# All streamed products with stationary weights, column tiles in pairs over two banks, and a feature-major residual

## The chip, the cores and the metric

One core of a Trainium2 chip runs the kernel. The metric is the device time of one execution in microseconds (us), smaller is better; the time shown is the median of three runs.

## What is computed

The kernel runs two layers on 256 tokens with 2048 features. Each layer is FFN, mixer, FFN, each on an RMS-normed input and added to the residual. The mixer of layer 0 (GDN) is a gated delta rule with 8 heads beside a multi-window pool; that of layer 1 (MLA) is latent attention with 16 heads.

```python
def swiglu(h, w_gate, w_up, w_down):
    return (jax.nn.silu(h @ w_gate) * (h @ w_up)) @ w_down
...
    for layer in range(DEPTH):
        x = x + 0.5 * swiglu(rms_norm(x, ffn1_norm[layer]), ffn1_w_gate[layer], ffn1_w_up[layer], ffn1_w_down[layer])
        h = rms_norm(x, mix_norm[layer])
        i = layer // 2
        if layer % 2 == 0:
            x = x + delta_pool_mixer(h, hyb_w_in[i], gdn_conv[i], gdn_a_log[i], gdn_dt_bias[i],
                                     gdn_out_norm[i], pool_w[i], pool_scale[i], hyb_w_out[i])
        else:
            x = x + mla_mixer(h, positions, mla_w_in[i], mla_q_norm[i], mla_kv_norm[i], mla_w_q_up[i],
                              mla_w_kv_up[i], mla_q_head_norm[i], mla_k_head_norm[i], mla_w_out[i])
        x = x + 0.5 * swiglu(rms_norm(x, ffn2_norm[layer]), ffn2_w_gate[layer], ffn2_w_up[layer], ffn2_w_down[layer])
```

The FFN width is 4096. All data are float32.

## The kernel before

Every large product is made in fp32r with both operands split: a high part (rounded to fp32r) and a low part (the rest), and three of the four partial products are summed: high with high, weight high with activation low, weight low with activation high. The weights stream from HBM in 1 MB slabs, `raw` (SyncE's queue, three buffers). `piece` makes of 1024 columns a high part on ScalarE (`whi`, a cast, L174) and a low part on VectorE (`wlo`, a subtraction, L175), with four buffers each.

There are two kinds of product. In the FFN and in the mixers' output projections (`columns`, `rows`) the activations are stationary: for each of 16 or 32 input tiles k and each 512 output columns there are six matmuls 512 wide (three partial products, two blocks of 128 tokens, one PSUM bank for each block). The results are token-major, and so is the residual `x[j]`, four tiles of [128, 2, 512]. Since the next product wants features on the partitions, PE transposes the FFN's hidden values (L458, eight per 512 columns) and, for the next norm, the residual (L336). In the mixers' input projections (`gemm`, `mm3`) the weights are stationary: for each k and 128 output columns there are three matmuls 256 wide into one bank, and the results are feature-major. `SKEW` and `PAD` set the distance of these operands' addresses.

The norm's gain is applied as `xg` is written (L158 on ScalarE and L159 on VectorE, high and low part). The factor 1/rms is taken from sums of squares that ScalarE accumulates per token (L309), and is applied to the results: as a per-token scale `r2` in the FFN (L134, L451), as the tile `R` in the mixers, made by one small matmul (`end_norm`).

A scheduler orders the instructions of each engine by a model of when each is ready, so the order on an engine is not the order of the code. Chains of small steps (heads, transposes) are spread between the streamed matmuls by a clock that counts PE's work (`ch.poll`, `LAG`).

Of the kernel before, what the change touches and what calls it, by code (L numbers as in the profile page):

```python
# [18 lines left out]
P = 128  # L19
# [6 lines left out]
PAD = 288  # L26
SKEW = 16
# [72 lines left out]
class Builder:  # L100
    def __init__(self, ctx, tc, ins, out):
        self.ctx, self.tc, self.nc, self.i, self.out = ctx, tc, tc.nc, ins, out
        self.act_set = None
        self.last_table = None
        pool = lambda name, bufs, **kw: ctx.enter_context(tc.tile_pool(name=name, bufs=bufs, **kw))
        self.cst = pool("cst", 1)
        self.xp = pool("xp", 1)
        self.wp = pool("wp", 4)
        self.tp = pool("tp", 2)
        self.ps = pool("ps", 1, space=PSUM)  # L110
        self.n = 0
        self.skew = 0
        self.ch = Chains()
# [52 lines left out]
    def piece(self, raw, h, step=1024):  # L166

        hi, lo = (
            self.wp.tile([P, 1024 + 64], F32R, tag=tag, bufs=4, name=self.nm(tag))[:, self.skew : self.skew + 1024]
            for tag in ("whi", "wlo")  # L170
        )
        for c in range(0, 1024, step):
            src, d = raw[:, h + c : h + c + step], slice(c, c + step)
            self.last_cast = self.nc.scalar.copy(hi[:, d], src)  # L174
            self.nc.vector.tensor_tensor(lo[:, d], src, hi[:, d].bitcast(F32), op=ALU.subtract)  # L175
        return hi, lo

    def weights(self, *aps):

        for ap in aps:  # L180
            n = ap.shape[1]
            for s0 in range(0, n, 2048):
                sz = min(2048, n - s0)
                raw = self.raw_tile()
                self.nc.sync.dma_start(raw[:, :sz], ap[:, s0 : s0 + sz])
                for h in range(0, sz, 1024):
                    yield self.piece(raw, h)
# [7 lines left out]
    def gemm(self, ps, stream, acts, wide=True):  # L195

        K = len(acts)
        for k0 in range(0, K, 8):
            self.gemm_piece(ps, next(stream), acts, k0, wide)

    def gemm_piece(self, ps, piece, acts, k0, wide=True):
        hi, lo = piece
        for k in range(k0, k0 + 8):
            w = slice((k - k0) * P, (k - k0 + 1) * P)
            self.ch.wait(lambda: acts[k] is not None)
            self.last_mm = self.mm3(ps, hi[:, w], lo[:, w], acts[k], k == 0, k == len(acts) - 1, wide)
            self.ch.poll()

    def mm3(self, ps, wh, wl, act, first, last, wide):
        if wide:  # L210
            if last:
                self.mm(ps[:, 0:256], wl, act[:, 0, :], start=False, stop=False)
            m = self.mm(ps[:, 0:512], wh, act.rearrange("p a t -> p (a t)"), start=first, stop=last)
            if not last:
                self.mm(ps[:, 0:256], wl, act[:, 0, :], start=False, stop=False)
        else:
            self.mm(ps[:, 0:256], wh, act[:, 0, :], start=first, stop=False)
            self.mm(ps[:, 0:256], wh, act[:, 1, :], start=False, stop=False)
            m = self.mm(ps[:, 0:256], wl, act[:, 0, :], start=False, stop=last)
        return m  # L220
# [56 lines left out]
    def warm_up(self):  # L277

        z = self.tmp([P, 512], "sq", 1)[:, 0:S]
# [6 lines left out]
    def load_rest(self):  # L286
        nc = self.nc
        nc.sync.dma_start(self.ca, self.i["ca"])
        self.behind(nc.scalar.copy(self.ones_r, self.ones), self.last_cast)
        for j in range(4):  # L290
            self.feed_squares(j, self.last_cast)
        self.norm_factor()

    def begin_norm(self, gain):
        self.gain = gain
        self.xg = [None] * KT
        self.ss = self.tmp([P, 2, 4], "ss", 2)

    def feed_part(self, d, src):

        t = self.xp.tile([P, 2, S], F32R, tag=f"xg{d}", name=self.nm("xg"))
        self.split_hi_lo(t, src, self.gains[:, self.gain, d : d + 1])
        self.xg[d] = t

    def feed_squares(self, j, earlier=None):

        for t in range(2):
            sq = self.tmp([P, 512], "sq", 1)
            a = self.nc.scalar.activation(sq, self.x[j][:, t, :], AF.Square, accum_out=self.ss[:, t, j : j + 1])  # L309
            if earlier is not None:  # L310
                self.behind(a, earlier)

    def norm_factor(self):

        nc = self.nc
        tot = self.tmp([P, 2], "tot", 1)
        nc.vector.tensor_reduce(tot, self.ss, axis=AX.X, op=ALU.add)
        self.r2 = self.tmp([P, 2], "r2", 1)
        self.rsqrt(self.r2, tot, 1.0 / D, True, "rt")
        self.dg = self.tmp([P, 2, P], "dg", 1)  # L320
        for t in range(2):
            nc.vector.tensor_scalar(self.dg[:, t, :], self.ident, self.r2[:, t : t + 1], None, op0=ALU.mult)

    def feed_norm(self, j):

        yield 1.2 * LAG
        self.feed_squares(j)
        if j == 3:
            self.norm_factor()
        x = self.x[j]  # L330
        for h in range(2):
            ps = self.psum("aux")
            for n in range(2):
                for t in range(2):
                    c = (2 * h + n) * P
                    self.nc.tensor.transpose(ps[:, (2 * n + t) * P : (2 * n + t + 1) * P], x[:, t, c : c + P], self.ident)  # L336
                    self.ch.clock += P / 2.4
            for n in range(2):
                self.feed_part(4 * j + 2 * h + n, ps[:, n * S : n * S + S])
            if h == 0:  # L340
                yield 0.5 * LAG

    def end_norm(self, after):

        ps = self.psum("aux")
        m = self.nc.tensor.matmul(ps[:, :S], self.ones, self.dg.rearrange("p a t -> p (a t)"), start=True, stop=True)
        self.behind(m, after)
        R = self.tp.tile([P, S], F32, tag="R", bufs=1, name=self.nm("R"))
        self.nc.scalar.copy(R, ps[:, :S])
        return R  # L350

    def rows(self, ps, hi, lo, act, first, last):

        blk = [slice(0, P), slice(P, 2 * P)]
        for part, w in ((0, hi), (0, lo), (1, hi)):
            end = last and part == 1
            for t in range(2):
                self.last_mm = self.mm(ps[t], act[:, part, blk[t]], w, start=first and w is hi and part == 0, stop=end)

    def columns(self, stream, acts):  # L360

        K = len(acts)
        ps = [self.psum("mm") for _ in range(2)]
        for k in range(K):
            if k % 2 == 0:
                piece = next(stream)
            hi, lo = (w[:, 512 * (k % 2) : 512 * (k % 2) + 512] for w in piece)
            self.ch.wait(lambda: acts[k] is not None)
            self.rows(ps, hi, lo, acts[k], k == 0, k == K - 1)
            self.ch.poll()  # L370
        return ps

    def project(self, slabs, acts, half, after):

        st = self.weights(*[slabs[j] for j in range(4)])
        for j in range(4):
            ps = self.columns(st, acts)
# [820 lines left out]
```

## Time and profile before

| | |
|---|---|
| median of three runs | 2829.64 us (2829.23 to 2829.73) |
| profiled execution | 2829.35 us, span 2827.3 us |
| PE busy | 2819.3 us of the span |
| DVE, ACT, POOL busy | 1555.1, 1360.2 and 57.4 us |
| granted clock | full in all 40 slices |
| read from HBM | 509.84 MB, 181 GB/s over the span |

PE is TensorE, DVE VectorE, ACT ScalarE, POOL GpSimd. Matmuls overlap on PE: the recorded time of one contains the filling of the array, so what a matmul costs is the distance from one start to the next (the pitch), not its recorded duration.

### The profile page before, as it was taken

The numbers are of one execution on the slowest core, as the hardware profiler recorded it, in microseconds if no ns is written. First come the engines' busy times: TensorE is split into PE (matmuls) and PEld (weight loads), VectorE is DVE, ScalarE is ACT, GpSimd is POOL, SyncE is SP. The second block draws the span as 40 slices with busy tenths as digits, with TensorE's granted clock in tenths as the row PEclk, the third lists the DMA queues.
The fourth block names the chain that finished last, engine by engine and source line by source line (L and its number), as shares of the span: only waits on it lengthen the run. The fifth ranks groups of instructions, "written<-read, shape, count | busy, mean of one in ns | idle before, by whom it ended". The sixth has DMA issues, their size and how long they took to land.

```text
span 2827.3 us, 35453 instructions
## 1 busy us (share of the span) xinstructions
PE 2819.3 (100%) x14398; PEld 2392.2 (85%) x14398; DVE 1555.1 (55%) x1893; ACT 1360.2 (48%) x1836; POOL 57.4 (2%) x97
## 2 busy tenths in 40 slices
PE   9999999999999999999999999999999999999999
PEld 8888888899998888888888888888999788888887
DVE  5445454576785545455454544545677555445444
ACT  6444444475465444444444444444578554444433
POOL 0000000000000000000000000000122000000000
PEclk9999999999999999999999999999999999999999
DMA  7555555545245555555555555555533455555554
GB/s 285 194 181 191 193 190 188 185 151 173 97 165 183 190 191 183 191 193 190 184 192 193 182 191 191 188 189 191 184 127 113 149 193 183 191 191 187 189 208 146
DMA packets 76500, 514.35 MB, mean 182 GB/s; under 512 B 10801, under 2 KB 11569, under 8 KB 15537
## 3 DMA queue, kind: packets, MB, share of 16 engines
q1 hardware_dynamic: 74464, 508.85, 52.5%
q8 instruction: 112, 1.84, 0.3%
q0 software_dynamic: 576, 2.10, 0.2%
q10 hardware_dynamic: 1296, 1.15, 0.1%
q14 instruction: 52, 0.42, 0.0%
HBM read 509.84 MB, written 2.10 MB: 181 GB/s over the span
## 4 chain that ended last, share of the span: by engine, by line
PE 98%; issue 1%; ACT 0%; DVE 0%; POOL 0%; DMA 0%; ACTq 0%; DVEq 0%; POOLq 0%
PE mm L193 91%; PE aux L193 4%; PE aux L458 1%; PE aux L336 1%; PE aux L701 0%; PE aux L1022 0%; PE aux L284 0%; ACT whi L174 0%; DMA cg<-in_cg 0%; ACT sq L309 0%; POOL osq L228 0%; PE aux L741 0%; ACT L129 0%; ACT sg L134 0%; ACTq L509 0%
## 5 line engine op out<-in xcount | busy, mean ns | idle before, releaser
L175 DVE TENSOR_TENSOR wlo<-raw,whi 128x1024 fp32r<-128x1024 f32 (+1 forms) x962 | 1175.2, 1222 | 1154.9 <-ACT whi L174 1153.4
L174 ACT CAST whi<-raw 128x1024 fp32r<-128x1024 f32 (+1 forms) x962 | 1007.9, 1048 | 1255.4 <-PE mm L193 1225.4
L193 PE MATMUL mm<-whi,xg 128*128 128x512 f32 x4096 | 1111.9, 391 | 0.0
L193 PEld LDWEIGHTS mm<-whi,xg 128*128 128x128 f32 x4096 | 764.3, 188 | 156.6 <-ACT whi L174 0.4
L193 PE MATMUL mm<-wlo,xg 128*128 128x512 f32 x2048 | 631.6, 389 | 0.0
L193 PE MATMUL mm<-whi,g 128*128 128x512 f32 x2048 | 554.8, 390 | 0.0
L193 PEld LDWEIGHTS mm<-wlo,xg 128*128 128x128 f32 x2048 | 384.4, 188 | 80.4 <-DVE wlo L175 0.4
L193 PEld LDWEIGHTS mm<-whi,g 128*128 128x128 f32 x2048 | 382.6, 188 | 78.0
L193 PE MATMUL mm<-wlo,g 128*128 128x512 f32 x1024 | 315.7, 389 | 0.0
L193 PE MATMUL mm<-xg,whi 128*128 128x256 f32 x1568 | 283.0, 283 | 0.6 <-ACT xg L158 0.5
L193 PEld LDWEIGHTS mm<-xg,whi 128*128 128x128 f32 x1568 | 239.9, 188 | 2.1 <-ACT xg L158 0.9
L193 PEld LDWEIGHTS mm<-wlo,g 128*128 128x128 f32 x1024 | 192.2, 188 | 40.3
L193 PE MATMUL mm<-xg,wlo 128*128 128x256 f32 x784 | 218.7, 279 | 0.0
L193 PEld LDWEIGHTS mm<-xg,wlo 128*128 128x128 f32 x784 | 148.3, 189 | 0.0
L193 PE MATMUL mm<-whi,o 128*128 128x512 f32 x256 | 72.3, 395 | 0.0
L228 POOL TENSOR_TENSOR sq<-sqf,sq 128x256 fp32r<-128x256 f32 x49 | 45.2, 928 | 1309.3 <-ACT sq L227 1296.3
L134 ACT ACTIVATE sg<-mm,r 128x512 f32<-128x512 f32 x64 | 40.6, 684 | 44.9 <-PE mm L193 44.9
L158 ACT ACTIVATE xg<-aux,gains 128x256 fp32r<-128x256 f32 x80 | 37.1, 471 | 36.9 <-DVE xg L159 26.2
L193 PEld LDWEIGHTS mm<-whi,o 128*128 128x128 f32 x256 | 47.0, 188 | 9.0
L462 ACT CAST g<-aux 128x512 fp32r<-128x512 f32 x64 | 37.3, 585 | 23.9 <-PE aux L458 23.9
L451 DVE SCALAR_TENSOR_TENSOR sg<-mm,r,sg 128x512 f32<-128x512 f32 x64 | 45.1, 746 | 5.8 <-PE mm L193 5.8
L159 DVE SCALAR_TENSOR_TENSOR xg<-aux,gains,xg 128x256 fp32r<-128x256 f32 x80 | 38.0, 481 | 16.6 <-ACT xg L158 16.6
(264 smaller groups left out, 1609.4 us busy)
## 6 DMA issues: line engine op xcount, KB each, us to landing
raw<-in_w1d SPq DMA_DIRECT2D x64, 1024.0 KB, 4.7
raw<-in_w2g SPq DMA_DIRECT2D x64, 1024.0 KB, 4.8
raw<-in_w2u SPq DMA_DIRECT2D x64, 1024.0 KB, 4.8
raw<-in_w2d SPq DMA_DIRECT2D x64, 1024.0 KB, 4.7
raw<-in_w1g SPq DMA_DIRECT2D x62, 1024.0 KB, 4.9
raw<-in_w1u SPq DMA_DIRECT2D x62, 1024.0 KB, 4.8
raw<-in_wqk SPq DMA_DIRECT2D x16, 1024.0 KB, 4.8
raw<-in_wgo SPq DMA_DIRECT2D x16, 1024.0 KB, 4.8
```

The lines of the kernel that those rows point to most:

```text
L134: a = nc.scalar.activation(out, in_, func, **kw)
L158: nc.scalar.activation(dst[:, 0, :], src, AF.Copy, scale=scale)
L159: nc.vector.scalar_tensor_tensor(dst[:, 1, :], src, scale, dst[:, 0, :].bitcast(F32), op0=ALU.mult, op1=ALU.subtract)
L174: self.last_cast = self.nc.scalar.copy(hi[:, d], src)
L175: self.nc.vector.tensor_tensor(lo[:, d], src, hi[:, d].bitcast(F32), op=ALU.subtract)
L193: return self.nc.tensor.matmul(out, lhsT, rhs, start=start, stop=stop)
L228: nc.gpsimd.tensor_tensor(dst[:, 1, :], sq, dst[:, 0, :].bitcast(F32), op=ALU.subtract)
L336: self.nc.tensor.transpose(ps[:, (2 * n + t) * P : (2 * n + t + 1) * P], x[:, t, c : c + P], self.ident)
L451: nc.vector.scalar_tensor_tensor(sg[:, t, :], ps[t], self.r2[:, t : t + 1], sg[:, t, :], op0=ALU.mult, op1=ALU.mult)
L458: nc.tensor.transpose(pt[:, (2 * n + t) * P : (2 * n + t + 1) * P], sg[:, t, c : c + P], self.ident)
L462: nc.scalar.copy(flat(0), pt)
```

## The change

All streamed products now keep the weights stationary. Two tiles of 128 output columns go together, A and B, each with a bank of its own. For each input tile k, `step` issues four matmuls: the high weights of A and of B against both parts of the activation at once (512 columns, parts side by side), then the low weights of A and of B against the high part (256 columns, into the first half of the bank); for the last k the low ones come first. High and low part of a piece lie 64 bytes apart in their tiles (`SIDE_A`, `SIDE_B`).

The halves of a bank are put together afterwards: `joined` copies one half to SBUF on ACT, adds the other on DVE and multiplies by `R` there. Results are feature-major everywhere, and so is the residual: 16 tiles of [128, 256], each updated by two DVE operations (`add_residual`). The transposes of hidden values and of the residual are gone, and with them the per-token scales. The sum of squares runs into a tile `acc`: for 14 of the 16 tiles on POOL (a multiplication and an addition each), for the last two on ACT and DVE; `end_norm` sums it over partitions by a matmul and takes the root of 128x256 values. In the opening of the first FFN, 256 gate and 256 up columns are made while the inputs arrive, where before it was 512 and 512; there the squares of six tiles run on POOL and of ten on ACT and DVE. The up-projections of the MLA heads (`wup`) go in pairs too, with two 512-wide casts per piece (`both_sides`), and the rotary parts of two pairs of heads are projected at once. The output is stored by ACT's DMA queue.

```diff
-PAD = 288
-SKEW = 16
+EXTRA = 64
+SIDE_A = (16, 0)
+SIDE_B = (0, 16)
+SIDE_V = (48, 48)
...
+    def split(self, hi, lo, src):
+        self.last_cast = self.nc.scalar.copy(hi, src)
+        self.nc.vector.tensor_tensor(lo, src, hi.bitcast(F32), op=ALU.subtract)
+    def piece(self, raw, h, side=SIDE_A):
+        hi, lo = (t[:, c : c + 1024] for t, c in zip(self.weight_tiles(), side))
+        self.split(hi, lo, raw[:, h : h + 1024])
...
+    def both_sides(self, raw, h):
+        tiles = self.weight_tiles()
+        out = []
+        for c, ats in ((0, SIDE_B), (512, [512 + SIDE_A[0], 512 + EXTRA + SIDE_A[1]])):
+            hi, lo = (t[:, o : o + 512] for t, o in zip(tiles, ats))
+            self.split(hi, lo, raw[:, h + c : h + c + 512])
+            out.insert(0, (hi, lo))
+        return out
+    def paired_weights(self, slabs):
+        for u in range(0, len(slabs), 2):
+            two = slabs[u : u + 2]
+            for c in range(0, two[0].shape[1], 2048):
+                raws = [self.raw_tile() for _ in two]
+                for raw, ap in zip(raws, two):
+                    self.nc.sync.dma_start(raw, ap[:, c : c + 2048])
+                for h in (0, 1024):
+                    yield [self.piece(raw, h, side) for raw, side in zip(raws, (SIDE_A, SIDE_B))]
...
+    def step(self, ps, ws, act, first, last):
+        whole = act.rearrange("p a t -> p (a t)")
+        def high():
+            for o, (hi, lo) in zip(ps, ws):
+                self.last_mm = self.mm(o, hi, whole, start=first, stop=last)
+        def low():
+            for o, (hi, lo) in zip(ps, ws):
+                self.mm(o[:, 0:S], lo, act[:, 0, :], start=False, stop=False)
+        for f in ((low, high) if last else (high, low)):
+            f()
+    def joined(self, out, ps, R):
+        self.nc.scalar.copy(out, ps[:, S : 2 * S])
+        self.nc.vector.tensor_tensor(out, ps[:, 0:S], out, op=ALU.add)
+        self.nc.vector.tensor_tensor(out, out, R, op=ALU.mult)
...
+    def feed_squares(self, d, pool, earlier=None):
+        nc = self.nc
+        eng = nc.gpsimd if pool else nc.vector
+        dst = self.acc if d == 0 else self.tmp([P, S], "sq")
+        if pool:
+            eng.tensor_tensor(dst, self.x[d], self.x[d], op=ALU.mult)
+        else:
+            a = nc.scalar.square(dst, self.x[d])
             if earlier is not None:
                 self.behind(a, earlier)
+        if d > 0:
+            eng.tensor_tensor(self.acc, self.acc, dst, op=ALU.add)
+    def feed_norm(self, d):
+        self.feed_parts(d)
+        self.feed_squares(d, d < KT - 2)
...
-        m = self.nc.tensor.matmul(ps[:, :S], self.ones, self.dg.rearrange("p a t -> p (a t)"), start=True, stop=True)
+        m = self.nc.tensor.matmul(ps[:, :S], self.ones, self.acc, start=True, stop=True)
...
-        self.nc.scalar.copy(R, ps[:, :S])
+        self.rsqrt(R, ps[:, :S], 1.0 / D, True)
...
-    def rows(self, ps, hi, lo, act, first, last):
-        blk = [slice(0, P), slice(P, 2 * P)]
-        for part, w in ((0, hi), (0, lo), (1, hi)):
-            end = last and part == 1
-            for t in range(2):
-                self.last_mm = self.mm(ps[t], act[:, part, blk[t]], w, start=first and w is hi and part == 0, stop=end)
-    def columns(self, stream, acts):
-        K = len(acts)
-        ps = [self.psum("mm") for _ in range(2)]
-        for k in range(K):
-            if k % 2 == 0:
-                piece = next(stream)
-            hi, lo = (w[:, 512 * (k % 2) : 512 * (k % 2) + 512] for w in piece)
-            self.ch.wait(lambda: acts[k] is not None)
-            self.rows(ps, hi, lo, acts[k], k == 0, k == K - 1)
-            self.ch.poll()
-        return ps
+    def add_residual(self, d, ps, half):
+        x = self.x[d]
+        for c in (slice(S, 2 * S), slice(0, S)):
+            if half:
+                self.nc.vector.scalar_tensor_tensor(x, ps[:, c], 0.5, x, op0=ALU.mult, op1=ALU.add)
+            else:
+                self.nc.vector.tensor_tensor(x, ps[:, c], x, op=ALU.add)
...
+        st = self.paired_weights([slabs[d] for d in range(KT)])
+        for d in range(0, KT, 2):
+            for e, ps in enumerate(self.pair(st, acts)):
+                self.add_residual(d + e, ps, half)
+                after(d + e)
...
+                    for k0 in range(0, 4, n):
+                        nc.sync.dma_start(x[:, k0 : k0 + n, :], self.i["x"][:, 4 * c + k0 : 4 * c + k0 + n, :])
+                        k = slice(512 * c + P * k0, 512 * c + P * (k0 + n))
+                        part = lambda t, o: t[:, o : o + 1024].rearrange("p (f k) -> p f k", f=2)[:, :, P * k0 : P * (k0 + n)]
+                        for w, src in enumerate((wg, wu)):
+                            nc.sync.dma_start(part(raw, 1024 * w), src[0:2, :, k].rearrange("f p k -> p f k"))
+                        for m in range(k0, k0 + n):
+                            self.feed_parts(4 * c + m)
+                        ws = []
+                        for w, side in enumerate((SIDE_A, SIDE_B)):
+                            hi, lo = (part(t, o) for t, o in zip(tiles[w], side))
+                            self.split(hi, lo, part(raw, 1024 * w))
+                            ws.append((hi, lo))
+                        for m in range(n):
+                            d = 4 * c + k0 + m
+                            for f in range(2):
+                                cols = slice(P * m, P * m + P)
+                                self.step(ps[f], [(hi[:, f, cols], lo[:, f, cols]) for hi, lo in ws], xg[d], d == 0, d == KT - 1)
...
+            def gated(pg, pu):
+                t, u = (gp.tile([P, S], F32, tag=n, bufs=3, name=self.nm(n)) for n in ("t", "u"))
+                self.joined(t, pg, R)
+                self.table(SILU, t, t, AF.Silu)
+                self.joined(u, pu, R)
+                nc.vector.tensor_tensor(u, u, t, op=ALU.mult)
+                gt = gp.tile([P, 2, S], F32R, name=self.nm("g"))
+                self.split_hi_lo(gt, u)
+                return gt
```

The order of PE in the first FFN, between two input tiles; `mm` is a bank, `xg` the activation. Before:

```order
L193 MATMUL mm_1671<-whi_1725,xg_194 128x512
L193 MATMUL mm_1672<-whi_1725,xg_194 128x512
L193 MATMUL mm_1671<-whi_1725,xg_197 128x512
L193 MATMUL mm_1672<-whi_1725,xg_197 128x512
L193 MATMUL mm_1671<-wlo_1726,xg_197 128x512
L193 MATMUL mm_1672<-wlo_1726,xg_197 128x512
L193 MATMUL mm_1671<-whi_1725,xg_197 128x512
```

After:

```order
L205 MATMUL mm_3302<-xg_168,whi_3294 128x512
L205 MATMUL mm_3303<-xg_168,whi_3298 128x512
L205 MATMUL mm_3302<-xg_168,wlo_3295 128x256
L205 MATMUL mm_3303<-xg_168,wlo_3299 128x256
L205 MATMUL mm_3302<-xg_171,whi_3294 128x512
```

Six matmuls of 512 columns for four tiles' worth of 128 columns have become four of 512, 512, 256 and 256 for two tiles.

The order of DVE where one group of output columns of a down projection ends and the next begins; `x` is the residual, `wlo` the low part of a piece of weights, `xg` the next norm's input. Before:

```order
L175 TENSOR_TENSOR wlo_3222<-raw_3219,whi_3221 128x1024
L381 SCALAR_TENSOR_TENSOR x_272<-mm_2855,x_272 128x512
L381 SCALAR_TENSOR_TENSOR x_272<-mm_2856,x_272 128x512
L175 TENSOR_TENSOR wlo_3238<-raw_3219,whi_3237 128x1024
L175 TENSOR_TENSOR wlo_3256<-raw_3253,whi_3255 128x1024
L159 SCALAR_TENSOR_TENSOR xg_3196<-aux_3191,gains,xg_3196 128x256
L159 SCALAR_TENSOR_TENSOR xg_3199<-aux_3191,gains,xg_3199 128x256
L175 TENSOR_TENSOR wlo_3272<-raw_3253,whi_3271 128x1024
L159 SCALAR_TENSOR_TENSOR xg_3213<-aux_3208,gains,xg_3213 128x256
L159 SCALAR_TENSOR_TENSOR xg_3216<-aux_3208,gains,xg_3216 128x256
```

After:

```order
L172 TENSOR_TENSOR wlo_3951<-raw_3946,whi_3950 128x1024
L172 TENSOR_TENSOR wlo_3955<-raw_3947,whi_3954 128x1024
L361 SCALAR_TENSOR_TENSOR x_159<-mm_3772,x_159 128x256
L361 SCALAR_TENSOR_TENSOR x_159<-mm_3773,x_159 128x256
L361 SCALAR_TENSOR_TENSOR x_159<-mm_3772,x_159 128x256
L361 SCALAR_TENSOR_TENSOR x_159<-mm_3773,x_159 128x256
L172 TENSOR_TENSOR wlo_3993<-raw_3946,whi_3992 128x1024
L160 SCALAR_TENSOR_TENSOR xg_3932<-x_159,gains,xg_3932 128x256
L160 SCALAR_TENSOR_TENSOR xg_3940<-x_159,gains,xg_3940 128x256
L172 TENSOR_TENSOR wlo_3997<-raw_3947,whi_3996 128x1024
```

and POOL beside it, after (it had no instruction in the down projections before):

```order
L336 TENSOR_TENSOR sq_4121<-x_159 128x256
L342 TENSOR_TENSOR acc_3561<-acc_3561,sq_4121 128x256
L336 TENSOR_TENSOR sq_4129<-x_159 128x256
L342 TENSOR_TENSOR acc_3561<-acc_3561,sq_4129 128x256
L336 TENSOR_TENSOR sq_4307<-x_216 128x256
```

The residual's update went from two operations of 512 columns to four of 256, the two `xg` of a group stand between the two pieces of weights that the second quarter of the next pair needs, and POOL squares the same `x` and adds it to `acc`.

The order of ACT at the end of the opening; `sq` are the squares of the first norm, `t` and `u` the first hidden values. Before:

```order
L174 CAST whi_424<-raw_360 128x1024
L289 CAST ones_r<-ca 128x128
L309 ACTIVATE sq_444,ss_87<-x_186 128x512
L309 ACTIVATE sq_446,ss_87<-x_186 128x512
L309 ACTIVATE sq_448,ss_87<-x_272 128x512
L174 CAST whi_487<-raw_485 128x1024
```

After:

```order
L171 CAST whi_423<-raw_419 128x1024
L338 ACTIVATE sq_363<-x_216 128x256
L338 ACTIVATE sq_366<-x_273 128x256
L338 ACTIVATE sq_369<-x_273 128x256
L239 COPY t_392<-mm_91 128x256
L338 ACTIVATE sq_372<-x_273 128x256
L338 ACTIVATE sq_375<-x_273 128x256
L239 COPY u_393<-mm_92 128x256
L239 COPY t_406<-mm_93 128x256
L239 COPY u_407<-mm_94 128x256
L171 CAST whi_427<-raw_420 128x1024
L171 CAST whi_465<-raw_419 128x1024
```

The two casts `whi_423` and `whi_427` belong to the two sides of one step; squares and copies of the opening's four banks now stand between them.

## Rows read from the trace of the kernel before

**Rows 1.** The page: busy us of each engine, and the chain that ended last.

```profile
PE 2819.3 (100%) x14398; PEld 2392.2 (85%) x14398; DVE 1555.1 (55%) x1893; ACT 1360.2 (48%) x1836; POOL 57.4 (2%) x97
PE 98%; issue 1%; ACT 0%; DVE 0%; POOL 0%; DMA 0%; ACTq 0%; DVEq 0%; POOLq 0%
```

**Rows 2.** Windows: stretch, then busy us and count by engine, clock, DMA share, GB/s.

```profile
100.00:200.00 100.00, 100.00 (x452) 82.86 (x451) 49.80 (x47) 42.88 (x45) 0.00 (x0) 1.00 0.56 188
...
540.00:845.00 305.00, 303.05 (x2475) 292.40 (x2474) 224.48 (x430) 185.65 (x309) 9.71 (x40) 1.00 0.44 147
...
2060.00:2188.00 128.00, 128.00 (x968) 115.98 (x967) 99.49 (x218) 104.54 (x272) 33.82 (x39) 1.00 0.35 120
```

**Rows 3.** Chain in order of time, two FFN stretches: start us, us, what.

```profile
1075.45 42.20 PE mm L193 x186
1119.91 42.20 PE mm L193 x186
```

**Rows 4.** Groups of PE by shape: count, then busy us and mean ns.

```profile
L193 PE MATMUL mm<-xg,whi 128*128 128x256 f32 x1568 | 283.0, 283 | 0.6 <-ACT xg L158 0.5
...
L458 PE MATMUL aux<-ca,sg 128*128 128x128 f32 x256 | 38.4, 272 | 0.2 <-DVE sg L451 0.2
...
L193 PE MATMUL mm<-q,whi 128*128 128x256 f32 x192 | 37.1, 289 | 0.0
...
L336 PE MATMUL aux<-ca,x 128*128 128x128 f32 x160 | 23.9, 272 | 0.0
...
L193 PE MATMUL mm<-kv,whi 128*128 128x256 f32 x128 | 23.3, 281 | 0.0
```

**Rows 5.** Timeline of PE, start of the GDN mixer: start us, us, instructions.

```profile
542.16 0.28 PE L193 MATMUL mm<-xg,wlo 128*128 128x256 f32 x1
542.29 0.60 PE L336 MATMUL aux<-ca,x 128*128 128x128 f32 x4
...
542.96 0.28 PE L193 MATMUL mm<-xg,wlo 128*128 128x256 f32 x1
...
546.22 0.38 PE L193 MATMUL mm<-xg,whi 128*128 128x256 f32 x1 [0.55 <-ACT xg L158]
```

**Rows 6.** Timeline of PE later in the GDN input projection.

```profile
553.61 3.86 PE L193 MATMUL aux<-xg,h 128*32 128x512 f32 x16
557.31 0.41 PE L193 MATMUL mm<-xg,whi 128*128 128x256 f32 x2
...
557.90 0.28 PE L193 MATMUL mm<-xg,wlo 128*128 128x256 f32 x1
...
560.62 0.28 PE L193 MATMUL mm<-xg,wlo 128*128 128x256 f32 x1
...
601.23 0.28 PE L193 MATMUL mm<-xg,wlo 128*128 128x256 f32 x1
...
603.71 0.28 PE L193 MATMUL mm<-xg,wlo 128*128 128x256 f32 x1
```

**Rows 7.** Groups of ACT and DVE by shape: busy us, mean ns.

```profile
L174 ACT CAST whi<-raw 128x1024 fp32r<-128x1024 f32 x958 | 1005.7, 1050 | 1254.6 <-PE mm L193 1225.4 <-issue 16.1 <-DMA raw<-in_w1u 9.3
...
L155 ACT CAST o<-aux 128x256 fp32r<-128x256 f32 x16 | 6.1, 380 | 3.3 <-PE aux L193 3.3
...
L175 DVE TENSOR_TENSOR wlo<-raw,whi 128x1024 fp32r<-128x1024 f32 x958 | 1172.6, 1225 | 1154.2 <-ACT whi L174 1152.8
...
L159 DVE SCALAR_TENSOR_TENSOR xg<-aux,gains,xg 128x256 fp32r<-128x256 f32 x80 | 38.0, 481 | 16.6 <-ACT xg L158 16.6
...
L542 DVE TENSOR_TENSOR cb<-mm,R 128x256 f32<-128x256 f32 x24 | 10.2, 423 | 14.2 <-PE mm L193 14.2
```

**Rows 8.** Timeline of POOL, and of DVE beside it at 809 us.

```profile
809.00 1.70 POOL L228 TENSOR_TENSOR osq<-sqf,osq 128x256 fp32r<-128x256 f32 x2 [1.20 <-ACT osq L227]
...
809.14 0.96 DVE L156 TENSOR_TENSOR dec<-dif,dec 128x256 fp32r<-128x256 f32 x1
810.03 0.97 DVE L821 TENSOR_TENSOR cb<-cb 128x269 f32<-128x269 f32 x1
...
2099.96 0.72 POOL L228 TENSOR_TENSOR sq<-sqf,sq 128x256 fp32r<-128x256 f32 x1 [1.40 <-ACT sq L227]
```

More of the change, by code (lines that the diff above doesn't have):

```diff
@@ L164, in raw_tile @@
         return self.wp.tile([P, 2048], F32, tag="raw", bufs=3, name=self.nm("raw"))
[L166 to L175, printed above, removed]
-        return hi, lo
@@ L178, in weights, with weight_tiles @@
[L178 to L187, printed above, removed]
+    def weight_tiles(self):
+        return [self.wp.tile([P, 1024 + EXTRA], F32R, tag=tag, bufs=4, name=self.nm(tag)) for tag in ("whi", "wlo")]
@@ L197, in gemm, with pair @@
+    def pair(self, stream, acts):
         K = len(acts)
+        ps = None
         for k0 in range(0, K, 8):
[L199 to L204, printed above, removed]
-            self.ch.wait(lambda: acts[k] is not None)
-            self.last_mm = self.mm3(ps, hi[:, w], lo[:, w], acts[k], k == 0, k == len(acts) - 1, wide)
-            self.ch.poll()
@@ L209, in mm3 @@
[L209 to L220, printed above, removed]
+            pieces = next(stream)
@@ L286, in load_rest @@
     def load_rest(self):
[L287 to L292, printed above, removed]
+        self.nc.sync.dma_start(self.ca, self.i["ca"])
+        last = self.last_cast
+        self.behind(self.nc.scalar.copy(self.ones_r, self.ones), last)
+        for d in range(KT):
+            self.feed_squares(d, d < 6, last)
     def begin_norm(self, gain):
@@ new lines, in ffn @@
+            early = opening() if start else []
+            st = self.paired_weights([w[f] for f in range(len(early), NF) for w in (wg, wu)])
+            g, R = [], None
+            if early:
+                R = self.end_norm(self.last_mm)
+            for f in range(NF):
+                ps = early.pop(0) if early else self.pair(st, xg)
+                if R is None:
+                    R = self.end_norm(self.last_mm)
+                g.append(gated(*ps))
+            self.project(wd, g, True, after)
@@ L809, in gdn @@
             df = []
-            for n in range(2):
-                ps = unit()
+            for n, ps in enumerate(units()):
                 ch.wait(lambda: heads[n]["done"] and (len(pools) < 2 or pools[-2]["done"]))
@@ L966, in mla @@
         for tag, gain in (("kv", kvg), ("q", qg)):
-            for n in range(4):
-                ch.spawn(latent(tag, n, unit(), gain), delay=LAG)
+            for n in (0, 2):
+                for e, t in enumerate(units()):
+                    ch.spawn(latent(tag, n + e, t, gain), delay=LAG)
                 if tag == "kv" and n == 0:
```

288 lines of the change are left out of this document (95 added, 193 removed).

## The prediction

> **What bounds the kernel now.** I read the page first: PE is busy 2819.3 of 2827.3 us and carries 98% of the chain that ended last [rows 1]. So only two things count: the time of PE's own work, and any wait of PE that the change brings in. The windows give the room that the others have. In an FFN stretch of 100 us DVE works 49.8 us and ACT 42.9; in the GDN mixer DVE works 224 of 305 us; in the MLA mixer's up-projections DVE works 99 and ACT 105 of 128 us [rows 2]. PE had no wait in that last stretch, but its helpers were near 80%.
>
> **The streamed products.** The number of streamed columns stays. A unit (one input tile k, 128 output columns) costs 768 columns before: 1.5 matmuls of 512 in the FFN and output projections, three of 256 in the mixers' inputs. After, it is one of 512 and one of 256. The FFN has 4 x 3 x 512 units, the two output projections 512: 6656 units. The mixers have (1568 + 192 + 128) / 2 = 944 [rows 4].
> - A 512-wide matmul takes 42.20 / 186 = 0.2269 us [rows 3].
> - A 256-wide matmul has two prices in this trace. From 601.23 to 603.71 us seven triples take 2.48 us, 0.354 each, 0.118 a matmul. From 557.90 to 560.62 us eight triples take 2.72, 0.340 each, 0.1133 a matmul, and this stretch begins right behind the 512-wide matmuls at 553.61 [rows 6]. In the new pattern every two narrow ones follow two wide ones, so I take 0.1133, the row it is nearest to.
> - FFN and outputs: 6656 x (0.2269 + 0.1133 - 1.5 x 0.2269) = 0 us. At 0.118 it is +31.
> - Mixers: 944 x (0.340 - 0.354) = **-13.2 us**; where a stretch already ran at 0.340 there is no gain, so the ends are -13 and 0.
> - Upper bound for the wide ones: the 16 matmuls at 553.61 have the same `xg` as the moving operand and take 3.70 / 16 = 0.231 us [rows 6]. 7600 x 0.004 = +31 us.
>
> **The transposes.** Two FFN stretches of the chain start 44.46 us apart [rows 3]; 192 matmuls at 0.2269 are 43.56. The missing 0.90 us are eight transposes and what they disturb. 256 / 8 = 32 such groups [rows 4]: -28.8. In the norms, four transposes stand between two low-part matmuls 0.80 us apart, 542.16 to 542.96, where 0.354 is usual [rows 5]: 0.446 us, 160 / 4 = 40 groups [rows 4], -17.8. Together **-46.6 us**.
>
> **New work on PE and around the norms.** Six sums over partitions replace six small factor matmuls, and a root of 128x256 values replaces one of 128x2. The trace has no such operation; ends 0 and 0.55 us each (the wait at the mixer's start, 546.22 [rows 5]); I take 0.4: **+2.5**.
>
> **The opening** covers 256 + 256 columns in half of the PE time, with the same 16 inputs to split. By the order shown, ACT now has squares and four copies of banks between the two casts of one step. The copies wait for the opening's last matmul; four at 0.38 us [rows 7] and the cast of 1.05 come before PE's next work, 2.6 us. Feeding the inputs faster costs as much again. **+5**; ends 0 and 15.
>
> **Starts of the mixers.** PE waited 0.55 us at 546.22 for ACT [rows 5]. The second side's cast (1.05 us) now queues behind the same small casts and DMA issues on ACT. Four copies or casts later is about 2.5 us at each of the two mixers: **+5**; ends 0 and 8.
>
> **Ends of pairs in projections that feed a norm.** There are five such projections with eight pairs each, 35 ends inside them. Count from the last matmul of a pair, by the order shown. The next piece's buffers come free there; its B side's low part is first needed after 8 x 0.680 + 2 x 0.227 + 0.113 = 6.0 us. DVE does four residual updates (0.48 each, some 0.08 less back to back: until 1.7), `wlo` A (1.22: until 2.9), two `xg` (until 3.75) and `wlo` B (until 5.0) [rows 7]. That would be in time. But POOL now squares and adds the same tiles, four operations. At 809 us POOL and DVE have operations on SBUF at once and alternate: two POOL operations take 1.70 us instead of 0.72 each, and two DVE ones 0.96 and 0.97 where 0.42 is usual for this size [rows 7, 8]. With three POOL operations fitted in, at 0.55 each, and a start 0.3 later, B ends at 6.9: 0.9 us late. If DVE goes first each time it is 0; if a POOL operation delays `wlo` A too and all four fall in, 1.5. I take 0.6, nearer to the alternation that the rows show: 35 x 0.6 = **+21**; ends 0 and 52. DVE is the engine that PE then waits for; behind the late `wlo` wait the next two, which have slack.
>
> The Trainium skill, page "SBUF — State Buffer", section "SBUF: two separate sides", says that a DVE operation with two SBUF inputs and a GpSimd operation that reads SBUF hold one shared port pair exclusively, and the loser waits for the whole instruction. The trace agrees, with 0.96 us instead of 0.42. It speaks against putting the squares on POOL beside the subtractions; by it the term is the +21 above, and without it 0, the sum 21 us lower.
>
> **MLA's up-projections.** 40 projected tiles get an ACT copy (0.38) and one more DVE operation (0.42) each [rows 7], and 20 pieces are cast in two halves (I take 0.2 more each): ACT 105 + 19 = 124, DVE 99 + 20 = 119 of a stretch in which PE needs 126. Ends: 0 if queues fill all gaps; if ACT keeps the 23 idle us it has now, 124 + 23 - 126 = 21. Middle: **+10**. The GDN mixer's DVE gets 40 such operations on 224 of 305 us; **+3**, ends 0 and 8.
>
> **At nothing.** In the FFN's up stretches a period of two tiles is 16 x 0.680 = 10.9 us; DVE has four `wlo` and six small operations, 7.5 us, ACT four casts and four small ones, 5.8; the order leaves the last `wlo` about 1 us early. Without this cover, 1 us would cost 126. At the start of the MLA output projection the last heads have half the time (16 x 0.68 us instead of 16 x 1.36), but in the order the second pair's matmuls stand in these gaps; without them some 10 us.
>
> **Sum**, against the profiled execution's 2829.35 us (0.29 below the median): -46.6 - 13.2 + 0 + 2.5 + 5 + 5 + 21 + 10 + 3 = -13.3, so **2816 us**.
>
> **Rivals.**
> 1. A clean stream: DVE keeps ahead of POOL and ACT fills its gaps, so that the +21 and +10 are nothing. For it: the helpers' mean load in the down projections stays near half. Against it: the rows at 809 us. 2816 - 31 = 2785.
> 2. A slower stream, on the other side: the narrow matmuls stay at 0.118 (as in most of the GDN input stretch), 7600 x 0.0047 = +36, 2852; or the wide ones take 0.231, 2847. It is slower than before from a narrow pitch of 0.1133 + 13.3 / 7600 = 0.115 us. For it: 601 to 604 us; against it: 557 to 561 us, behind wide ones.
> 3. DVE and POOL collide fully: 1.5 us an end, 35 x 0.9 = +31, 2847. It turns the sign at 0.6 + 13.3 / 35 = 0.98 us an end.
>
> **How the numbers follow.** About 0.2% (5.7 us) is what a measurement of this kernel tells from no change. Forecast 0.42, rival 1 0.25, rival 2 0.18, rival 3 0.15. The forecast's own terms reach from 2800 to 2832, about seven tenths of it below 2824: 0.29 + 0.25 of faster, 0.54. Same gets 0.10 of the forecast and 0.06 of the rivals' milder forms, 0.16; slower 0.30. The range takes in both rivals: 2780 to 2850.
>
> **What would show it.** Right: no transposes; triples of 0.340 in the windows of FFN and mixers; waits of PE for `wlo` some 35 times at the ends of pairs, longest where a POOL operation lies beside it; one wait of 2 to 3 us near 31 us. Wrong: narrow matmuls at 0.118 apart, PE idle within FFN up stretches, or PE idle for more than 20 us between the heads of MLA.

## The result: 38 us slower

The changed kernel takes 2867.94 us (2865.5 to 2869.91, four runs) where the kernel before takes 2829.68 (2829.23 to 2830.24): a ratio of 1.0135 (95% interval 1.0117 to 1.0152). The forecast was 2816 us. The direction and the range (2780 to 2850) were both missed.

The page of the changed kernel, to be held against [rows 1]:

```profile
PE 2844.0 (99%) x16378; PEld 2465.1 (86%) x16378; DVE 1838.1 (64%) x2789; ACT 1426.5 (50%) x2251; POOL 193.7 (7%) x239
...
PEclk9999999999999999999999999999999999999999
...
PE 93%; DVE 2%; issue 2%; ACT 1%; DMA 1%; POOL 0%; SPq 0%; DVEq 0%; ACTq 0%; POOLq 0%
```

PE is still the bound, at full clock, and now has 2844 us of work instead of 2819, with the transposes gone. So the time did not go into waits of PE first of all; its own matmuls became dearer. Windows of three FFN up stretches show by how much (columns as in [rows 2], PE alone):

```profile
100.00:200.00 100.00, 100.00 (x573) 1.00 0.52 186
1000.00:1100.00 100.00, 100.00 (x573) 1.00 0.53 189
2400.00:2500.00 100.00, 100.00 (x573) 1.00 0.52 185
```

573 matmuls in 100 us are 573 / 4 steps: 0.698 us a step of four, where the sum had 2 x (0.2269 + 0.1133) = 0.680. The timeline shows a step as it repeats (start us, us, instructions):

```profile
130.28 0.63 PE L205 MATMUL mm<-xg,whi 128*128 128x512 f32 x2
130.75 0.40 PE L205 MATMUL mm<-xg,wlo 128*128 128x256 f32 x2
130.98 0.63 PE L205 MATMUL mm<-xg,whi 128*128 128x512 f32 x2
```

The pairs of wide matmuls start 0.70 us apart. By the single starts the four cost 231, 236, 118 and 115 ns. But the step of 0.680 exists too. It stands in the first down projection until a pair ends at 436 us:

```profile
435.21 0.39 PE L205 MATMUL mm<-g,wlo 128*128 128x256 f32 x2
435.43 0.61 PE L205 MATMUL mm<-g,whi 128*128 128x512 f32 x2
435.89 0.63 PE L205 MATMUL mm<-g,wlo 128*128 128x256 f32 x4
436.35 1.10 PE L205 MATMUL mm<-g,whi 128*128 128x512 f32 x4
437.28 0.40 PE L205 MATMUL mm<-g,wlo 128*128 128x256 f32 x2
...
437.99 0.40 PE L205 MATMUL mm<-g,wlo 128*128 128x256 f32 x2
```

From 435.21 to 435.89 is 0.68 us; from 437.28 to 437.99 it is 0.71, and then 0.70 for the rest of the stretch. Between them lies the pair's end, where `step` gives the low products first: four narrow ones in a row (x4), then four wide ones (the last two of the pair and the first two of the next). The same turn from short to long stands at every pair's end of the FFNs that a short step reaches in this trace, but for the first pair's end of an up stretch, where the norm's sum stands too. The stream of matmuls has two paces at the same clock, a short step and a long one; the expectations below call them the fast and the slow state.

Over the whole trace I added up, for each streamed matmul, what its start-to-start distance has above 0.2267 or 0.1133 us. Small excesses (under 30 ns, the pace) are 69.3 us after and 11.4 before, so +57.9. Larger ones (waits) are 35.3 after and 21.4 before, +13.9. The streamed columns themselves, at these two prices, come to 2605.8 us before and 2605.5 after.

### The profile page after: what moved, and what is told of

Its sections match the earlier page's. It is cut to its first block, busy times and chain, and to the rows that moved or that the text cites. A ratio compares the mean times of both kernels' runs of the same rounds, so it can differ in the third digit from the quotient of the medians.

```text
span 2865.4 us, 40867 instructions
## 1 busy us (share of the span) xinstructions
PE 2844.0 (99%) x16378; PEld 2465.1 (86%) x16378; DVE 1838.1 (64%) x2789; ACT 1426.5 (50%) x2251; POOL 193.7 (7%) x239
## 4 chain that ended last, share of the span: by engine, by line
PE 93%; DVE 2%; issue 2%; ACT 1%; DMA 1%; POOL 0%; SPq 0%; DVEq 0%; ACTq 0%; POOLq 0%
PE mm L205 89%; PE aux L205 4%; DVE wlo L172 1%; POOL sq L254 0%; ACT whi L171 0%; DMA raw<-in_wu 0%; DMA x<-in_x 0%; DMA raw<-in_w1u 0%; PE aux L648 0%; DVE cb L773 0%; DMA raw<-in_wmo 0%; DVE xg L160 0%; DVE x L361 0%; DVE y L492 0%; PE aux L980 0%
## 5 line engine op out<-in xcount | busy, mean ns | idle before, releaser
L205 PE MATMUL mm<-xg,whi 128*128 128x512 f32 x4880 | 1523.6, 396 | 4.6 <-DVE x L361 3.1
L205 PEld LDWEIGHTS mm<-xg,wlo 128*128 128x128 f32 x4880 | 895.3, 188 | 203.9 <-DVE wlo L172 6.3
L205 PE MATMUL mm<-xg,wlo 128*128 128x256 f32 x4880 | 955.0, 279 | 3.9 <-DVE wlo L172 3.9
L205 PEld LDWEIGHTS mm<-xg,whi 128*128 128x128 f32 x4880 | 758.2, 188 | 24.9 <-ACT whi L171 7.3
L205 PE MATMUL mm<-g,whi 128*128 128x512 f32 x2048 | 636.9, 394 | 0.0
L205 PEld LDWEIGHTS mm<-g,wlo 128*128 128x128 f32 x2048 | 380.1, 188 | 89.9 <-DVE wlo L172 3.1
L205 PE MATMUL mm<-g,wlo 128*128 128x256 f32 x2048 | 401.6, 280 | 0.0
L205 PEld LDWEIGHTS mm<-g,whi 128*128 128x128 f32 x2048 | 313.2, 188 | 2.8
L205 PE MATMUL mm<-o,whi 128*128 128x512 f32 x256 | 80.7, 397 | 0.0
L342 POOL TENSOR_TENSOR acc<-acc,sq 128x256 f32<-128x256 f32 x70 | 80.2, 1146 | 5.3
```

Source lines behind the costliest of these rows:

```text
L205: return self.nc.tensor.matmul(out, lhsT, rhs, start=start, stop=stop)
L342: eng.tensor_tensor(self.acc, self.acc, dst, op=ALU.add)
```

## The experiments

**Is it the order at a pair's end?** `e1_order`:

```diff
-        for f in ((low, high) if last else (high, low)):
-            f()
...
+        high()
+        low()
```

The flag that ends the sum in a bank moves to the new last matmul, here and in every run below with another order.

> The high products come first for every k, the last one too (the changed kernel reverses the last k of a pair). Theory A, the stream has a fast state (a step of four matmuls in 0.680 us) and a slow one (0.700), and the reversal throws it into the slow one, since there four 256-wide matmuls follow each other and the next weights' addresses stand the other way round: the steps run at 0.680 us in the FFN up stretches, some 55 to 65 us less, 2805 to 2812 us. Theory B, the slow state belongs to the mix of 512 and 256 columns itself, whatever the order at a pair's end: 0.700 us stays, 2863 to 2871 us.

Measured: 2853.06 us (2839.69 to 2865.67), ratio 1.0078 (1.0047 to 1.0109). Both numbers missed. The profile says why: the pace now holds through whole stretches, but not the same one in each.

```profile
100.00:200.00 100.00, 100.00 (x574) 1.00 0.49 187
1000.00:1100.00 100.00, 100.00 (x590) 1.00 0.52 196
2400.00:2500.00 100.00, 100.00 (x573) 1.00 0.50 190
```

590 matmuls are 0.678 us a step. All steps of the second FFN's up stretch are short (348.6 us for the stretch), all of the fourth FFN's are long (358.8). So the reversal drives a short pace into the long one, and without it the pace stays as it was when the stretch began. In the down projections it turned at waits for `wlo`, but not at all of them. Five waits of 0.30 to 0.36 us led from the short step into the long one; eight of 0.30 to 0.37 us did not, or for two steps only (among them all six in the third FFN); the five waits of 0.13 to 0.19 us in a long step all led back. Two equal waits with different outcomes:

```profile
444.18 0.80 PE L205 MATMUL mm<-g,wlo 128*128 128x256 f32 x2
444.81 0.62 PE L205 MATMUL mm<-g,whi 128*128 128x512 f32 x2
...
445.51 0.63 PE L205 MATMUL mm<-g,whi 128*128 128x512 f32 x2
```

```profile
1900.88 0.80 PE L205 MATMUL mm<-g,wlo 128*128 128x256 f32 x2
1901.52 0.62 PE L205 MATMUL mm<-g,whi 128*128 128x512 f32 x2
...
1902.19 0.62 PE L205 MATMUL mm<-g,whi 128*128 128x512 f32 x2
```

The step behind the first is 0.70 us, behind the second 0.67 to 0.68. The length of a wait alone does not decide. The five times lie at 2839.7, near 2853 (three) and at 2865.7, some 13 us apart.

**Do the addresses matter?** The offsets of high and low part, one set for each FFN, with the order of the changed kernel (`e2_sides`) and with that of `e1_order` (`e2b_sides_order`):

```diff
-                    yield [self.piece(raw, h, side) for raw, side in zip(raws, (SIDE_A, SIDE_B))]
+                    yield [self.piece(raw, h, side) for raw, side in zip(raws, sides)]
...
+SIDES = [(SIDE_A, SIDE_B), ((0, 0), (0, 0)), ((16, 16), (16, 16)), ((0, 16), (16, 0))]
```

> Order as in the changed kernel; the offsets of high and low part differ by FFN: first FFN as changed (64/0, 0/64 bytes for sides A and B), second all 0, third all 64, fourth exchanged (0/64, 64/0). Theory A: where a load's address goes with the running matmul decides: the up stretches (358.5 us each now) are slower in the second to fourth FFN, the fourth most, 360 to 380 us. Theory B: the offsets do nothing, all four up stretches 357 to 360 us (the first 363 with its opening).

> The four offsets by FFN of the run e2_sides, with the order of e1_order. Theory A: the first FFN at 0.680 us a step, the others slower, the fourth most. Theory B: all four at 0.700.

Four more sets followed in `e5_sides`, four in `e6_sides`, with the order of `e1_order`.

> Order as e1_order; offsets in bytes of high/low part for sides A, B, by FFN: (64/0, 64/64), (64/0, 64/0), (64/64, 64/0), (64/0, 0/0). Theory A': each of the four loads of a step has its own good offset, and a step costs 0.680 us plus some 5 to 10 ns for each load that stands wrong: 0.685 to 0.700, the same in every step of a stretch. Rival: the fast state exists only for the offsets of the changed kernel, all others lie at 0.693 to 0.702.

> As e5_sides with the offsets (0/0, 0/64), (0/64, 0/64), (0/0, 64/64), (64/64, 0/64) by FFN, and the same two expectations; if one set runs at 0.680 us in a whole up stretch with no slow state in its down stretch after waits, it is better than that of the changed kernel.

The mean step in the up stretch, in ns, from the trace:

| offsets high/low, A; B (bytes) | run | step |
|---|---|---|
| 64/0; 0/64 (as changed) | `e2_sides` | 700 |
| 0/0; 0/0 | `e2_sides` | 697 |
| 64/64; 64/64 | `e2_sides` | 694 |
| 0/64; 64/0 | `e2_sides` | 702 |
| 64/0; 0/64 | `e2b_sides_order` | **681** |
| 0/0; 0/0 | `e2b_sides_order` | 697 |
| 64/64; 64/64 | `e2b_sides_order` | 693 |
| 0/64; 64/0 | `e2b_sides_order` | 702 |
| 64/0; 64/64 | `e5_sides` | 703 |
| 64/0; 64/0 | `e5_sides` | 713 |
| 64/64; 64/0 | `e5_sides` | 707 |
| 64/0; 0/0 | `e5_sides` | 700 |
| 0/0; 0/64 | `e6_sides` | 700 |
| 0/64; 0/64 | `e6_sides` | 700 |
| 0/0; 64/64 | `e6_sides` | 707 |
| 64/64; 0/64 | `e6_sides` | 693 |

The four runs took 2862.5, 2862.2, 2895.9 and 2878.3 us (one each). The offsets do act, from 693 to 713 ns, and only the changed kernel's own set was seen at 680. That set ran at 680 in one run and at 700 in another, and each other set was seen in one or two executions only; so a short pace of another set may have gone unseen. The expectation of `e2b_sides_order` under Theory A came out set by set, though the same first FFN had run long in `e1_order`, so that it did so was in part chance. Neither expectation of `e5_sides` had the dear end right, none of its sets or of those of `e6_sides` ran at 680, and in `e2_sides` the third FFN came out faster (355.7 us for the stretch), which neither theory had. The last set's 693 are steps of 688 and 698 in turn. Single offsets do not add up by load; which rule the addresses follow stays open. In `e2b_sides_order` the first FFN ran the short step, and the order made no difference to the other three sets:

```profile
100.00:200.00 100.00, 100.00 (x590) 1.00 0.50 190
1000.00:1100.00 100.00, 100.00 (x577) 1.00 0.50 190
...
2400.00:2500.00 100.00, 100.00 (x572) 1.00 0.49 187
```

**What do POOL's squares cost?** `e3_nopool`:

```diff
-        self.feed_squares(d, d < KT - 2)
+        self.feed_squares(d, False)
```

> All squares after the opening on ACT and their sums on DVE, none on POOL. Theory C, the waits of PE at the ends of pairs (about 0.18 us each at 35 places) are the low parts that DVE makes late since POOL's squares keep it from SBUF: these waits go, 4 to 8 us less, 2860 to 2864 us. Rival D, DVE's own queue is late there, with two more sums in it the waits stay or grow: 2868 to 2880 us.

Measured: 2864.8 us, one run, between the two expected ranges and only 0.7 us below the lowest of the changed kernel's four. A pair's end in the changed kernel, DVE and POOL:

```profile
459.30 1.42 DVE L361 SCALAR_TENSOR_TENSOR x<-mm,x 128x256 f32<-128x256 f32 x4 [1.55 <-PE mm L205]
460.63 1.53 DVE L172 TENSOR_TENSOR wlo<-raw,whi 128x1024 fp32r<-128x1024 f32 x1
462.08 1.71 DVE L160 SCALAR_TENSOR_TENSOR xg<-x,gains,xg 128x256 fp32r<-128x256 f32 x2
463.72 1.75 DVE L172 TENSOR_TENSOR wlo<-raw,whi 128x1024 fp32r<-128x1024 f32 x1
```

```profile
460.46 0.61 POOL L336 TENSOR_TENSOR sq<-x 128x256 f32<-128x256 f32 x1 [18.59 <-DVE x L361]
461.15 1.60 POOL L342 TENSOR_TENSOR acc<-acc,sq 128x256 f32<-128x256 f32 x1
462.72 0.79 POOL L336 TENSOR_TENSOR sq<-x 128x256 f32<-128x256 f32 x1
463.59 0.80 POOL L342 TENSOR_TENSOR acc<-acc,sq 128x256 f32<-128x256 f32 x1
```

The two take turns, as in [rows 8]: the two `xg` need 1.71 us together, where one takes 0.48 [rows 7], and the second `wlo` 1.75 instead of 1.22, so it ends at 465.47. The waits of PE's weight loads for `wlo` (us, times, longest) in the changed kernel and then in `e3_nopool`:

```profile
PEld mm L205 <- DVE wlo L172: 16.2, 44, 2.4
```

```profile
PEld mm L205 <- DVE wlo L172: 6.3, 7, 2.4
```

37 waits with 9.9 us are gone: theory C holds for the waits. The time fell by some 3 us only, if one run can tell it. Counted by the starts of the matmuls, PE's waits fell by 5.5 us (29.8 from 35.3), and the pace cost 3.2 more (72.5 from 69.3): without the waits no pace turned to the short step in the down projections (all their steps are long, where the changed kernel has 8 to 26% short ones in the first three).

**Both edits**, `e4_order_nopool`:

> e1_order and e3_nopool together. In the trace of e1_order the state held through whole stretches and turned at waits of 0.13 us (slow to fast) and 0.30 us (fast to slow). Theory A with waits as the only other turning: without the waits at the pairs' ends the state turns less often, so an FFN whose up stretch is fast stays fast to its end; an execution still draws its state at stage starts: 2800 (all fast) to 2862 us (all slow), median near 2830, wider spread than before. Rival: the waits were not what turned it, the state changes inside down projections as often as in e1_order.

Measured: 2825.09 us (2810.78 to 2838.68, ten runs), ratio 0.9985 (0.996 to 1.001), so no difference from before that can be told. Median and spread are near what Theory A had. The ten times lie on three levels: 2838 (four), 2822 to 2826 (four) and 2811 (two). In the profiled one, at 2838.6, the first and fourth FFN run long steps nearly from begin to end and the second and third short ones; no pace turned inside a down projection, as Theory A had it. A long FFN costs some 10 us in its up and 5 in its down stretch (358.8 against 348.6 in `e1_order`, 180.5 against 175.4 here), near the distance of the levels, 13 to 14. So the levels fit two, one and no long FFN; only the one execution has a trace.

**Can an order lead back?** Since one order at the pair's end leads into the long step, others may lead out. `e7_turns` and `e8_turns` try four, each on two different FFNs, on top of `e4_order_nopool`:

```diff
+        n = range(len(ps))
+        order = [(high, e) for e in n] + [(low, e) for e in n]
+        if last and len(ps) == 2:
+            order = [order[q] for q in self.turn]
+        for f, e in order:
+            f(e)
```

> As e4_order_nopool, but at the last input tile of each pair the four matmuls go in another order, by FFN: (high A, low A, high B, low B), (high B, high A, low B, low A), (high A, high B, low B, low A), (high B, high A, low A, low B). The changed kernel's order there (low, low, high, high) leads into the slow state from either state. Theory A'': an order at the pair's end that puts loads at the wrong distance sets the state, the slow one or, for another order, the fast one: an up stretch is then wholly slow (358 us) or wholly fast (348 us) from its first pair on, in this run and in e8_turns alike. Rival: these orders leave the state as it was drawn at the stretch's start, so the same order shows the one state here and may show the other in e8_turns.

> The four orders of e7_turns on other FFNs: the third and fourth of them in the first and second FFN, the first and second in the third and fourth FFN. Theory A'': each order shows the same state as in e7_turns. Rival: it does not.

Measured: 2842.5 and 2830.4 us, one run each. By order (up stretches; long or short step by the trace):

| order at the last tile | `e7_turns` | `e8_turns` |
|---|---|---|
| high A, low A, high B, low B | long up to a pair's end, then short (682) | first pair short, second long, then short (681) |
| high B, high A, low B, low A | first pair short, second long, then short but for two or three steps behind each pair's end (683) | two pairs long, then the same (684) |
| high A, high B, low B, low A | first pair short, then long | short but for one to three steps behind each pair's end (684) |
| high B, high A, low A, low B | first pair long, second short, then long | two pairs short, then long |

Theory A'' holds for three of the four: the first two set the short step, the last sets the long one, in both runs, whatever came before; the third keeps what it finds. The last three give the same sequence of widths (512, 512, 256, 256) and yet set the short pace, keep it and set the long one; so it is not the widths alone that set it, but also which tile's weights, and with them which bank, come when. These two are not separated. The orders act so from the second pair's end of an up stretch on (in the first FFN, whose opening makes two pairs, soon after it), and not from the first, as expected. Two places of the third FFN in `e8_turns`, the first and the second pair's end:

```profile
1485.62 0.62 PE L208 MATMUL mm<-xg,whi 128*128 128x512 f32 x2
...
1486.30 0.39 PE L208 MATMUL mm<-xg,whi 128*128 128x512 f32 x1
...
1487.00 0.60 PE L356 MATMUL aux<-acc,ca 128*128 128x256 f32 x2
1487.24 0.82 PE L208 MATMUL mm<-xg,whi 128*128 128x512 f32 x2
1487.90 0.40 PE L208 MATMUL mm<-xg,wlo 128*128 128x256 f32 x2
...
1488.60 0.40 PE L208 MATMUL mm<-xg,wlo 128*128 128x256 f32 x2
...
1497.93 0.39 PE L208 MATMUL mm<-xg,whi 128*128 128x512 f32 x1
1498.16 0.28 PE L208 MATMUL mm<-xg,wlo 128*128 128x256 f32 x1
1498.28 0.40 PE L208 MATMUL mm<-xg,whi 128*128 128x512 f32 x1
1498.51 0.28 PE L208 MATMUL mm<-xg,wlo 128*128 128x256 f32 x1
1498.63 0.62 PE L208 MATMUL mm<-xg,whi 128*128 128x512 f32 x2
...
1499.31 0.61 PE L208 MATMUL mm<-xg,whi 128*128 128x512 f32 x2
```

The step is 0.68 us (1485.62, 1486.30) until the norm's sum, an fp32 matmul that the trace records as two (L356), stands at the first pair's end; behind it the step is 0.70 (1487.90, 1488.60). At the second pair's end wide and narrow stand in turn, and behind that it is 0.68 again (1498.63, 1499.31) to the stretch's end. The sum and the order act together there: with this order the second pair is long in all seven up stretches of the second to fourth FFN that have it in `e8_turns`, `e9_turn` and `e10_turn_nopool`, while with the order of `e1_order` and `e4_order_nopool` the pace before the sum was the pace behind it in all six. The next pair's end corrects it.

**The first order everywhere**, alone (`e9_turn`) and without POOL's squares (`e10_turn_nopool`):

```diff
+TURN = (0, 2, 1, 3)
...
+            order = [order[q] for q in TURN]
```

> The changed kernel with one edit: the four matmuls of a pair's last input tile go as high A, low A, high B, low B (it had low A, low B, high A, high B). In e7_turns and e8_turns this order led from the slow into the fast state at the first pair's end and kept it. Theory A'': every up stretch runs at 0.680 us a step from its second pair, in every execution; waits at pairs' ends in the projections may turn the state, and the next pair's end turns it back: 2806 to 2818 us, a spread under 5 us. Rival, the state is drawn by chance at each start whatever the order: a median of 2825 to 2855 us with a spread over 10 us.

> e9_turn with all squares after the opening on ACT and DVE, none on POOL. Theory A'' with theory C: also the waits at the pairs' ends are gone, 35 of some 0.2 to 0.4 us and what they turn: 2802 to 2812 us, 4 to 10 us under e9_turn. Rival: with the state held, POOL's waits hide or cost under 2 us, no difference.

Measured, beside 2829.84 for the kernel before: `e9_turn` 2820.72 us (2818.08 to 2821.9), ratio 0.9964 (0.995 to 0.9977); `e10_turn_nopool` 2811.16 us (2809.14 to 2812.11), ratio 0.9932 (0.992 to 0.9945). One edit of order takes 47 us off the changed kernel, the spread of five runs is under 4 us, and both are faster than the kernel before. `e9_turn` is 3 us above the upper end of what was expected, and its up stretches are short from the third pair on (but for single steps behind pairs' ends) and not from the second; `e10_turn_nopool` lies within its range. In `e9_turn` the waits for `wlo` still turn the pace in the down projections, some of them and each time only until the next pair's end: about a fifth of the steps are long in the first three of them, in `e10_turn_nopool` at most one behind each pair's end. So POOL's squares cost 9.6 us here, waits and pace together, as expected (4 to 10). The last kernel's page and windows:

```profile
PE 2790.0 (99%) x16378; PEld 2448.2 (87%) x16378; DVE 1811.5 (64%) x2854; ACT 1449.4 (52%) x2321; POOL 69.9 (2%) x104
```

```profile
100.00:200.00 100.00, 100.00 (x589) 1.00 0.50 190
1000.00:1100.00 100.00, 100.00 (x589) 1.00 0.51 193
2400.00:2500.00 100.00, 100.00 (x589) 1.00 0.51 191
```

PE's work is 54 us less than in the changed kernel (2844.0), with the same 16378 matmuls.

## Why the prediction was wrong, by its steps

**The price of the stream.** The step that failed is "0.1133, the row it is nearest to", and with it "0.2269". I took the best row for each width and let rival 2 spoil one of the two at a time (2852 or 2847). In the changed kernel both are spoiled together, 231 + 236 + 118 + 115 = 700 ns a step, and in 94 to 97% of the steps of the FFNs' up stretches and 73 to 100% of their down stretches: +58 us against the trace before. Of the 20 ns that a long step costs more, the two wide ones carry some 13 and the two narrow ones 6. The rows for it were at hand: 0.231 for wide ones with moving `xg`, and two prices of narrow ones in one stretch [rows 6]. The trace before even shows where the one price of narrow ones turns into the other, at four small matmuls put in between:

```profile
571.35 0.28 PE L193 MATMUL mm<-xg,wlo 128*128 128x256 f32 x1
...
571.69 0.28 PE L193 MATMUL mm<-xg,wlo 128*128 128x256 f32 x1
571.81 0.51 PE L193 MATMUL aux<-g,cg 128*128 128x8 f32 x4
...
573.55 0.28 PE L193 MATMUL mm<-xg,wlo 128*128 128x256 f32 x1
...
573.90 0.28 PE L193 MATMUL mm<-xg,wlo 128*128 128x256 f32 x1
```

A triple takes 0.34 us ahead of them and 0.35 behind them. Two prices in one stretch mean that something other than the shape decides, and I chose between them without asking what turns the one into the other. Nor did I read the one place where the new pattern breaks, the reversed last tile, as a possible cause, though the section on the change names it.

**The mixers' -13.2.** I took 0.354 for all triples. The excess of small size in the two input stages was 8.6 us in the trace before, not 13.2, and is 7.4 after. The GDN input stage went from 305.8 to 309.0 us, MLA's stayed at 184.1. The gain was not there.

**The transposes' -46.6** hold in the main. By the starts of the matmuls the transposes themselves took 36.9 us of the trace before; by the stretches below some 40 us came, if the output projections gave as much as the down projections. With the short step an up stretch takes 349.7 us in `e10_turn_nopool` (second FFN) where it took 355.7: 6.0 of the expected 7.2; in `e4_order_nopool`, whose pair ends are not turned, the same stretch takes 348.6, the whole 7.1. The down projections gave 2.4 each of 3.6.

**The opening's +5** was right in size and wrong in place. The first up stretch is 363.2 us, 4.4 more than the second, 358.8; before they were equal (355.6, 355.7). But the wait for ACT near 31 us did not come. The largest is for the low part at 16 us, while the inputs arrive:

```profile
16.37 0.50 PE L205 MATMUL mm<-xg,wlo 128*128 128x256 f32 x2 [1.97 <-DVE wlo L172]
```

**The starts of the mixers**, +5: 1.2 us each (at 549 and 2028), so +1 instead. The same wait stands at 1490, at the start of an FFN, for which the sum had no term.

**The pairs' ends**, +21: the mechanism was right and the size was off. POOL and DVE alternate, `wlo` B comes late, and `e3_nopool` removes just these waits: 9.9 us of the weight loads' and 5.5 us of the matmuls', where I had 21. The second `wlo` took 1.75 us, and PE waited about 0.2 us for it, not 0.6. The forecast had no term for what a wait does to the pace behind it.

**MLA's +10**: not there. In its window ACT works 103.3 and DVE 108.2 us, not 124 and 119:

```profile
2060.00:2188.00 128.00, 126.58 (x777) 106.86 (x776) 108.20 (x245) 103.27 (x282) 34.57 (x36) 1.00 0.37 129
```

The stage shifts by 25 us in the changed kernel, so the same window holds an earlier part of it; but its length did not change. The waits in the GDN stage grew by 4.2 us (10.9 from 6.7) for the +3; no run shows which change brought them. In all, waits grew by 13.9 us and other new work of PE by 3.7, where the sum had 46.5. These terms were too dark by some 30 us, and that hid nearly half of the 71 us by which the stream's two terms (0 and -13.2) were too low.

Rival 2 had the right side and the right place, a slower stream, with half the price. The chance of slower was 0.30.

## What to carry to other kernels

Where the trace shows two prices for one and the same instruction, find the row at which the one turns into the other before pricing a pattern made of it, and let both widths go wrong at once when bounding. In such a periodic stream of matmuls with weight loads, one irregular step at the end of each group set the dear pace for all steps to the next one, and another order of the same four instructions set the cheap one. Count matmuls in windows of 100 us; with the changed kernel's addresses two numbers (573, 589) told the pace of a stretch here. Times on levels 13 us apart fit a pace that is drawn anew in each execution; only one execution of each kernel has a trace, so that is not shown.

## What the runs showed of the hardware beyond that

At full granted clock a step of 512, 512, 256 and 256 columns with four weight loads ran at 680 ns or at 700 ns for hundreds of steps on end, with the same instructions and the same offsets. In the FFNs it turned within three steps of a wait, an irregular step or the start of a stretch, and nowhere else; but equal waits turned it at one place and not at another (five of thirteen near 0.30 us in `e1_order`). The distance of the high and low parts' addresses moved the mean step between 693 and 713 ns in the other sets. Why the two paces exist was not shown: no run separates the reads of the weights from those of the activations, or these from the banks. Four narrow ones in a row are not needed for the long one: the order high B, high A, low A, low B set it without them.
